# The first two column groups of a decoder's first feed-forward: weights as the resting operand, or activations

## The chip, the cores and the metric

The kernel runs on one core of a Trainium2 chip. The metric is the device time of one execution in microseconds (us), taken as the median over several executions. Beside it stands one execution that the hardware profiler recorded, with its own time and span.

## The reference

A two-layer decoder trunk on 256 tokens with a model width of 1024. Only its beginning matters here: the first half-step feed-forward of layer 0, whose inner width is 2816.

```python
def rmsnorm(x, g):
    xf = x.astype(jnp.float32)
    y = xf * lax.rsqrt(jnp.mean(xf * xf, axis=-1, keepdims=True) + EPS)
    return (y * g.astype(jnp.float32)).astype(x.dtype)

def swiglu_ffn(x, w_in, w_out):
    gate, up = jnp.split(x @ w_in, 2, axis=-1)
    return (jax.nn.silu(gate) * up) @ w_out
...
    for i in range(DEPTH):
...
        h = h + 0.5 * swiglu_ffn(rmsnorm(h, ffn1_norm[i]), ffn1_w_in[i], ffn1_w_out[i])
```

Everything else (the gated convolution, the shared keys and values, the sparse attention, the other feed-forwards) comes after it and is the same in both kernels.

## The kernel before

Every product is made in split precision: an operand is cut into a high part (rounded to the matmul type, `wh` for weights, the first 256 columns of an `xs` tile for activations) and a low part (what is left, `wl`, and the last 256 columns of `xs`). A product is high x high, low x high and high x low, added up in PSUM. ScalarE (ACT) casts the high parts, VectorE (DVE) subtracts to get the low ones. The inner dimension of 1024 is cut into eight tiles k = 0 to 7 of 128.

The instructions of each engine stand in the order in which the code is written: no scheduler moves them. So an engine that waits for one thing holds up all that stands behind it in its own queue. SP is the queue that issues nearly all DMAs, POOL adds up the squares for the norm.

Weights come as a stream `W`: `load` fetches 1 MB chunks of 2048 columns into three staging buffers `ws`; `high` and `low` cut half a chunk, a unit of 1024 columns, into `wh` and `wl`; `take`, `done` and `pump` hand units out, free them and prepare further ones, up to six ahead. For column groups a unit holds two k tiles, and a group of 256 inner features takes four units (gate and up together are 512 columns).

A feed-forward's first product is made in one of two ways.

- In `ffn_tokens` the activations rest in the array (128 tokens) and 512 weight columns move through it: per k tile two token tiles times three products, six matmuls. The result lies with tokens on partitions. `turned` applies the norm's factor per token (`rc`, from `Norm.cols`), SiLU and the gate, transposes blocks and writes them to DRAM; `placed` reads them back with features on partitions; `halved` splits them for the second product.
- For the first four tiles of 128 inner features the weights rest and the activations move: `first_tiles` makes three of them, k by k, while the input and the weights arrive in the pieces that `FIRST` and `THIRD` list; `ffn_in` makes the fourth from two units of the stream. Per tile, gate and up, and k this is one matmul of 512 columns (high weights on high and low activations) and one of 256. They need no transpose, but a factor per column (`First.rows`), sums of two halves (`total`) and an evaluation of their own (`ffn_evac`), which is woven into the groups that follow (`old`).

The column groups g = 2 to 10 then run in `ffn_tokens`, and `out_proj` follows. `NWARM` matmuls on a tile of ones run on TensorE (PE) before any input is there.

Of the kernel before, what the change touches and what calls it, by code (L numbers as in the profile page):

```python
# [9 lines left out]
F32 = mybir.dt.float32  # L10
# [6 lines left out]
P = 128  # L17
# [26 lines left out]
FROM = {"ffn1": (2, 0), "ffn2": (0, 0)}  # L44
# [25 lines left out]
def trunk(ctx, tc, A, out):  # L70
# [163 lines left out]
    w2st = mk([P, CHUNK], "ws", 3)  # L234
    came = 0
    for n, (lo, hi) in enumerate(zip(FIRST, FIRST[1:])):
        todo = [base[:, lo:hi]]
        if n in THIRD:
            todo.append(w2st[:, THIRD[n][0] * 2 * P:THIRD[n][1] * 2 * P])
        for dst in todo:  # L240
            m = P * dst.shape[1]
            (ac if came == FIRST[1] * P else sy).dma_start(dst, A["first"][came:came + m].rearrange("(p n) -> p n", p=P))
            came += m
# [4 lines left out]
    parts = {(f, g): kt8[:, g[0]:g[-1] + 1, T + f * 2 * P:T + (f + 1) * 2 * P].rearrange("p k (u m) -> p u k m", u=2)  # L248
             for f in range(2) for g in GROUPS}
    W.loaded = 3  # L250
# [122 lines left out]
    def times(r, R, n):  # L373
        ve.tensor_tensor(out=r, in0=r, in1=R[:, None, :].to_broadcast([P, n, T]), op=ALU.mult)

# [5 lines left out]

    def ffn_evac(r, R, hd):
        times(r, R, 2)
        yield
        s = t1()
        ac.activation(s, r[:, 0], AF.Silu)
        ve.tensor_tensor(out=s, in0=s, in1=r[:, 1], op=ALU.mult)
        yield
        split(s, hd)
# [12 lines left out]
    def ffn_in(xs, norm, sums):  # L402

        sums, hid, box, us, o = list(sums), [act() for _ in range(4)], [], W.take(2), bank2()
        a_pass([(o[:, x], us[x], xs, range(8)) for x in range(2)], mid=lambda: box.append(norm.rows()))
        W.done(2, False)
        sums.append(total(o, 2))
        W.pump()
        return hid, [ffn_evac(r, box[0], hd) for r, hd in zip(sums, hid)]

    def ffn_tokens(xs, norm=None, rc=None, bg=None, pre=None, n0=0, hid=(), old=()):

        hid, old, box, last = list(hid), list(old), [rc], NF // 2 - 1
# [6 lines left out]
        def turned(o):  # L420
            rc, tb = box[0], t2([P, 2, T])
            for tt in range(2):
                s = t1()
                ac.activation(s, o[:, tt, :T], AF.Silu, scale=rc[:, tt:tt + 1])  # L424
                ve.scalar_tensor_tensor(out=s, in0=o[:, tt, T:], scalar=rc[:, tt:tt + 1], in1=s, op0=ALU.mult, op1=ALU.mult)  # L425
                ve.transpose(tb[:, tt], s)  # L426
            d = mk([2, P, T], "turn", 3, pool=dr)
            sy.dma_start(d.rearrange("t p n -> p t n"), tb)
            return d

        def placed(d):
            ht = t2([P, 2, T])
            sy.dma_start(ht.rearrange("p f (c j) -> p f c j", j=32), d.rearrange("t (a i) (c f j) -> (i c) f (t a) j", i=32, f=2, j=32))
            return ht

        def halved(ht):
            for f in range(2):
                hd = act()
                split(ht[:, f], hd)
                hid.append(hd)  # L440

        ready, way = None, None
        for g in range(n0, last + 1):
            o = bank2()
            for k in range(8):
# [5 lines left out]
                for tt in range(2):  # L451
                    sh, sl = xs[k][:, tt * P:(tt + 1) * P], xs[k][:, T + tt * P:T + (tt + 1) * P]
                    pe.matmul(o[:, tt], sh, wh, start=(k == 0), stop=False)  # L453
                    pe.matmul(o[:, tt], sl, wh, start=False, stop=False)  # L454
                    pe.matmul(o[:, tt], sh, wl, start=False, stop=(k == 7))  # L455
                if k == 3 and ready is not None:
                    halved(ready)
                    ready = None
                if k == 5 and way is not None:
                    ready, way = placed(way), None  # L460
                if k == 7:
                    way = turned(o)
                    if g == last:
                        way = placed(way)
                if k % 2 == 1:
                    W.done()
                    if old and k % 4 == 1:
                        list(old.pop(0))
                    if bg is not None and k % 4 == 3:
                        bg(2 * g + k // 4)  # L470
        halved(ready)
        return hid, lambda: halved(way)

# [177 lines left out]
    sq = [t2([P, 2, T]) for _ in range(4)]  # L651

    def square(k):
        ac.activation(sq[k // 2][:, k % 2], h[k], AF.Square)

    def first_tiles():

        o = [bank2(), bank2()]
        oo, o = o, [[x[:, u] for u in range(2)] for x in o] + [[bank(), bank()]]
        w = [[mk([P, 2, 4, P], t, NBUF, F32R) for t in ("wh", "wl")] for _ in range(6)]  # L660

        def lows(f, src, g):
            wh, wl = w[2 * f + g[0] // 4]
            ks = slice(g[0] % 4, g[-1] % 4 + 1)
            ve.tensor_tensor(out=wl[:, :, ks], in0=src, in1=wh[:, :, ks].bitcast(F32), op=ALU.subtract)

        def highs(f, src, g, copy=ac.copy):
            copy(w[2 * f + g[0] // 4][0][:, :, g[0] % 4:g[-1] % 4 + 1], src)

        def product(f, k, u, x, c=slice(0, 512)):  # L670
            pe.matmul(o[f][u][:, c], w[2 * f + k // 4][x][:, u, k % 4], xs[k][:, c], start=k == x == c.start == 0, stop=(k == 7 and x == 1))

        def products(f, g):
            for x in range(2):
                for u in range(2):
                    for k in g:
                        product(f, k, u, x, slice(0, (2 - x) * T))

        def third(ks):
            g = range(*ks)  # L680
            src = w2st[:, ks[0] * 2 * P:ks[1] * 2 * P].rearrange("p (k u m) -> p u k m", u=2, m=P)
            highs(2, src, g)
            lows(2, src, g)

        def more(k):
            po.tensor_tensor(out=late if k > 1 else sq[0], in0=late if k > 2 else sq[0], in1=sq[k], op=ALU.add)

        def by_halves(k, mid):
            nm.high(k)
            highs(0, parts[0, (k,)], (k,), ve.tensor_copy)  # L690
            highs(1, parts[1, (k,)], (k,))
            nm.low(k)
            for f in range(2):
                lows(f, parts[f, (k,)], (k,))
            for c in (slice(0, T), slice(T, 512)):
                for f in range(2):
                    for u in range(2):
                        product(f, k, u, 0, c)
            mid()
            for f in range(2):  # L700
                for u in range(2):
                    product(f, k, u, 1, slice(0, T))

        by_halves(0, lambda: None)
        third(THIRD[1])
        square(0)
        products(2, (0,))
        by_halves(1, lambda: products(2, (1,)))
        square(1)
        for n, g in enumerate(GROUPS):  # L710
            if n < 2:
                continue
            for k in g:
                nm.tile(k, False)
            for f in range(2):
                highs(f, parts[f, g], g)
                lows(f, parts[f, g], g)
            for k in g:
                square(k)
            for f in range(2):  # L720
                products(f, g)
            if n == 2:
                third(THIRD[3])
            if n < 4:
                products(2, g)
            if g[-1] == 3:
                more(1)
        late = kt8[:, 6:8, 2 * T:]
        for k in (2, 3):
            more(k)  # L730
        po.tensor_tensor(out=nm.sq, in0=late[:, 0], in1=late[:, 1], op=ALU.add)
        third(THIRD[6])
        W.units += [None] * 6
        W.take(6)
        W.done(6, False)
        W.high()
        sums = [total(x, 2) for x in oo]
        products(2, GROUPS[-2] + GROUPS[-1])
        W.pump(1)
        r = t2([P, 2, T])  # L740
        for u in range(2):
            ac.copy(r[:, u], o[2][u][:, T:])
        for u in range(2):
            ve.tensor_tensor(out=r[:, u], in0=o[2][u][:, :T], in1=r[:, u], op=ALU.add)
        sums.append(r)
        W.pump(1)
        q = act()
        split(nm.sq, q)
        W.pump(2)
        return sums, q  # L750

    class First:
        def rows(self):
            pb = bank()
# [772 lines left out]
```

## Time and profile before

| what | value |
|---|---|
| median of 3 executions | 952.04 us (952.02 to 952.41) |
| the profiled execution's own time | 952.55 us |
| its span, first to last instruction | 950.8 us |
| what lies around the span | 1.75 us |
| busy share of PE, DVE, ACT, POOL | 100%, 70%, 57%, 14% |
| DMA moved over the span | 205.30 MB, mean 216 GB/s |

A busy PE is not the same as a PE at its peak: matmuls are pipelined, and a row's time for one matmul (some 390 ns) is longer than the step from one matmul to the next. Steps are read from the start times in the timeline. The profiled execution took 0.51 us more than the median of the runs.

### The profile page before, as it was taken

How to read it: one execution, taken by the hardware profiler on the slowest of the kernel's cores; microseconds unless marked ns; L12 is line 12 of the kernel's file. 1: busy time of each engine (PE TensorE's matmuls, PEld its weight loads, DVE VectorE, ACT ScalarE, POOL GpSimd, SP SyncE). 2: the span in 40 equal slices, each digit the busy share in tenths (PEclk: the TensorE clock that was granted, in tenths of full speed). 3: DMA queues.
4: the chain of work that ended last, by engine and by line, in shares of the span. 5: the costliest groups of instructions: out<-in, count | busy, mean ns of one | idle time of the engine just before them, and what ended most of it. 6: DMA issues, size and time to landing. Idle time of an engine off the chain costs nothing.

```text
span 950.8 us, 12961 instructions
## 1 busy us (share of the span) xinstructions
PE 946.1 (100%) x4712; PEld 794.8 (84%) x4712; DVE 661.1 (70%) x1066; ACT 538.5 (57%) x903; POOL 136.1 (14%) x212
## 2 busy tenths in 40 slices
PE   9999999999999999999999999999999999999998
PEld 8888888888888888888888888888877888888887
DVE  6777666778886667747757676866679787766652
ACT  7755444555565455545647774754589765445540
POOL 2000000245520100001221022200238120000000
PEclk9999999999999999999999999999999999999999
DMA  8468877645546998777646876786510248989750
GB/s 312 178 221 250 278 233 266 216 172 210 178 160 234 257 274 272 237 272 221 220 152 218 254 244 238 257 278 192 201 59 30 105 177 252 280 268 280 254 214 23
DMA packets 149467, 205.30 MB, mean 216 GB/s; under 512 B 111467, under 2 KB 126443, under 8 KB 128796
## 3 DMA queue, kind: packets, MB, share of 16 engines
q1 hardware_dynamic: 149260, 204.22, 65.7%
q8 instruction: 37, 0.61, 0.2%
q10 hardware_dynamic: 144, 0.26, 0.1%
q14 instruction: 26, 0.21, 0.1%
HBM read 189.22 MB, written 14.71 MB: 214 GB/s over the span
## 4 chain that ended last, share of the span: by engine, by line
PE 99%; ACT 0%; DVE 0%; issue 0%
PE mm L453 16%; PE mm L455 16%; PE mm L454 16%; PE a L554 7%; PE mm L355 4%; PE a L355 4%; PE a L560 4%; PE mm L516 3%; PE mm L515 3%; PE mm L514 3%; PE mm L360 2%; PE a L613 2%; PE a L612 2%; PE a L611 2%; PE a L360 2%; PE mm L1225 1%
## 5 line engine op out<-in xcount | busy, mean ns | idle before, releaser
L183 DVE TENSOR_TENSOR wl<-ws,wh 128x1024 fp32r<-128x1024 f32 x318 | 392.6, 1255 | 201.7 <-ACT wh L166 193.2
L166 ACT CAST wh<-ws 128x1024 fp32r<-128x1024 f32 x318 | 326.5, 1048 | 207.8 <-DMA ws<-in_ffn_w_in_dram 89.7
L453 PE MATMUL mm<-wh,xs 128*128 128x512 f32 x672 | 262.6, 391 | 0.0
L455 PE MATMUL mm<-wl,xs 128*128 128x512 f32 x672 | 261.7, 389 | 0.0
L454 PE MATMUL mm<-wh,xs 128*128 128x512 f32 x672 | 261.5, 389 | 0.0
L455 PEld LDWEIGHTS mm<-wl,xs 128*128 128x128 f32 x672 | 126.1, 188 | 26.8 <-DVE wl L183 0.4
L454 PEld LDWEIGHTS mm<-wh,xs 128*128 128x128 f32 x672 | 126.2, 188 | 25.8
L453 PEld LDWEIGHTS mm<-wh,xs 128*128 128x128 f32 x672 | 126.2, 188 | 25.8
L315 POOL TENSOR_TENSOR sq<-sq,t 128x256 f32<-128x256 f32 x35 | 28.5, 815 | 373.7 <-ACT t L313 373.1
L424 ACT ACTIVATE t<-mm,rc 128x256 f32<-128x256 f32 x84 | 39.7, 473 | 53.9 <-DVE t L425 46.4
L554 PE MATMUL a<-act,wh 128*128 128x512 f32 x296 | 69.5, 390 | 0.0
L554 PEld LDWEIGHTS a<-act,wh 128*128 128x128 f32 x296 | 54.9, 188 | 11.0
L514 PE MATMUL mm<-wh,act 128*128 128x512 f32 x132 | 51.3, 389 | 0.0
L515 PE MATMUL mm<-wh,act 128*128 128x512 f32 x132 | 51.3, 389 | 0.0
L516 PE MATMUL mm<-wl,act 128*128 128x512 f32 x132 | 51.3, 389 | 0.0
L425 DVE SCALAR_TENSOR_TENSOR t<-mm,rc,t 128x256 f32<-128x256 f32 x84 | 40.4, 481 | 15.4 <-ACT t L424 12.1
L363 ACT CAST act<-t 128x256 fp32r<-128x256 f32 x96 | 34.7, 404 | 27.1 <-DVE t L789 19.4
L298 ACT ACTIVATE xs<-base 128x256 fp32r<-128x256 f32 x48 | 23.8, 504 | 42.6 <-DVE base L476 29.4
L364 DVE TENSOR_TENSOR act<-t,act 128x256 fp32r<-128x256 f32 x96 | 37.1, 423 | 6.4 <-ACT act L363 6.4
L426 DVE STREAM_TRANSPOSE t<-t 128x256 f32<-128x256 f32 x84 | 37.4, 446 | 3.0
L560 PEld LDWEIGHTS a<-act,wl 128*128 128x128 f32 x296 | 37.2, 191 | 1.0
L560 PE MATMUL a<-act,wl 128*128 128x256 f32 x296 | 37.5, 283 | 0.0
(292 smaller groups left out, 1194.4 us busy)
## 6 DMA issues: line engine op xcount, KB each, us to landing
ws<-in_ffn_w_in_dram SPq DMA_DIRECT2D x85, 1024.0 KB, 5.6
ws<-in_ffn_w_out_dram SPq DMA_DIRECT2D x44, 1024.0 KB, 6.0
ws<-in_conv_w_in_dram SPq DMA_DIRECT2D x12, 1024.0 KB, 4.6
turn<-t SPq DMA_DIRECT2D x42, 256.0 KB, 2.3
t<-turn SPq DMA_DIRECT2D x42, 256.0 KB, 7.1
ws<-in_w_kv_dram SPq DMA_DIRECT2D x6, 1024.0 KB, 5.7
ws<-in_conv_w_out_dram SPq DMA_DIRECT2D x4, 1024.0 KB, 5.1
ws<-in_attn_w_q_dram SPq DMA_DIRECT2D x4, 1024.0 KB, 5.5
```

Of the source, the lines that this page charges most:

```text
L166: ac.copy(h, src)
L183: ve.tensor_tensor(out=l, in0=src, in1=h.bitcast(F32), op=ALU.subtract)
L355: pe.matmul(o, u[0][:, k * P:(k + 1) * P], xs[k], start=(k == 0), stop=False)
L425: ve.scalar_tensor_tensor(out=s, in0=o[:, tt, T:], scalar=rc[:, tt:tt + 1], in1=s, op0=ALU.mult, op1=ALU.mult)
L453: pe.matmul(o[:, tt], sh, wh, start=(k == 0), stop=False)
L454: pe.matmul(o[:, tt], sl, wh, start=False, stop=False)
L455: pe.matmul(o[:, tt], sh, wl, start=False, stop=(k == 7))
L514: pe.matmul(o[:, tt], sh, wh, start=(k == 0), stop=False)
L515: pe.matmul(o[:, tt], sl, wh, start=False, stop=False)
L516: pe.matmul(o[:, tt], sh, wl, start=False, stop=(k == NF - 1))
L554: pe.matmul(o, run[k][0], lhs[k], start=(k == 0), stop=(k == last))
L560: pe.matmul(o[:, :T], run[k][1], lhs[k][:, :T], start=False, stop=(k == last))
```

## The change

The four special tiles go. The first two column groups (the same 512 inner features) are made with the activations resting, like all others, in a function `first_groups` that works k tile by k tile on both groups at once while input and weights arrive. `PIECES` lists the loads: group 0's weights stand beside the input in `base`, group 1's lie in two of the three `ws` buffers (`second`), and two pieces, not one, are issued from ACT's queue. The sum of squares is added up by POOL tile by tile, 128x256 each (`nm.squares`), and the factor per token is made once between the two groups (`nm.cols`) instead of at the end of group 2. After k = 5, 6 and 7 one unit of the stream is prepared in between (`W.pump(1)`). The evaluations of the two groups (`turned`) come right behind each; their `placed` and `halved` are woven into groups 2 and 3.

```diff
-GROUPS = ((0,), (1,), (2,), (3,), (4, 5), (6, 7))
...
-FIRST = [0, G_N + T, G_N + KW] + [G_N + (g[-1] + 1) * KW for g in GROUPS[1:]]
-THIRD = {1: (0, 2), 3: (2, 4), 6: (4, 8)}
+PIECES = ((0, 0, G_N + T, 0), (0, G_N + T, G_N + KW, 1), (1, 0, 1, 0), (0, G_N + KW, G_N + 2 * KW, 1), (1, 1, 2, 0),
+          (0, G_N + 2 * KW, G_N + 3 * KW, 0), (0, G_N + 3 * KW, G_N + 4 * KW, 0), (1, 2, 4, 0), (0, G_N + 4 * KW, G_N + 6 * KW, 0),
+          (1, 4, 6, 0), (0, G_N + 6 * KW, G_N + 8 * KW, 0), (1, 6, 8, 0))
...
-    w2st = mk([P, CHUNK], "ws", 3)
+    second = [mk([P, CHUNK], "ws", 3) for _ in range(2)]
...
+    for which, lo, hi, queue in PIECES:
+        dst = base[:, lo:hi] if which == 0 else second[lo // 4][:, lo % 4 * 512:lo % 4 * 512 + (hi - lo) * 512]
+        m = P * dst.shape[1]
+        (sy, ac)[queue].dma_start(dst, A["first"][came:came + m].rearrange("(p n) -> p n", p=P))
+        came += m
...
-    W.loaded = 3
+    W.loaded = 4
     W.load(4)
...
-    def first_tiles():
...
+    def first_groups():
+
+        o = [[x[:, tt] for tt in range(2)] for x in (bank2(), bank2())]
+        units = {}
+        W.units += [None] * 8
+        W.at = 8
...
+        lo, hi = slice(0, T), slice(T, 512)
+        for k in range(8):
+            if k < 2:
+                nm.high(k)
+                high(0, k, ve.tensor_copy, lo)
+                high(0, k, ac.copy, hi)
+                nm.low(k)
+                high(1, k)
+                low(0, k)
+                nm.squares(k)
+                low(1, k)
+                products(0, k, 0, lo)
+                products(0, k, 0, hi)
+                for x, g in ((1, 0), (0, 1), (1, 1), (2, 0), (2, 1)):
+                    products(g, k, x)
+            else:
+                nm.tile(k)
+                for g in range(2):
+                    high(g, k)
+                    low(g, k)
+                if k < 6:
+                    for g in range(2):
+                        for x in range(3):
+                            products(g, k, x)
+            if k == 3:
+                second[0] = None
+                W.load(5)
+            if k % 2 and k < 6:
+                for g in range(2):
+                    del units[g, k // 2]
+                W.done(2, False)
+            if k > 4:
+                W.pump(1)
+        d = []
+        for g in range(2):
+            for k in (6, 7):
+                for x in range(3):
+                    products(g, k, x)
+            del units[g, 3]
+            W.done(1, False)
+            if g == 0:
+                rc = nm.cols()
+            d.append(turned(o[g], rc))
+            W.pump(2)
+        second[1] = None
+        return rc, d
...
-    sums, parts_sq = first_tiles()
-    hid, old = ffn_in(xs, First(), sums)
-    hid, rest = ffn_tokens(xs, nm, n0=2, hid=hid, old=old)
+    rc, ways = first_groups()
+    hid, came = [], []
+    old = [lambda d=d: came.append(placed(d)) for d in ways] + [lambda: halved(came.pop(0), hid) for _ in ways]
+    hid, rest = ffn_tokens(xs, rc=rc, n0=2, hid=hid, old=old)
```

`high(g, k)` casts and `low(g, k)` subtracts 512 columns; `products(g, k, x)` is two matmuls of 512 columns, x = 0 high x high, 1 low activations, 2 low weights (`wl`). The host's layout of the first weights follows. Group 2 takes two single PSUM banks, since the two double ones hold groups 0 and 1.

Where the work on the last input tiles stands in ACT's queue, before: tiles 4 and 5 are cut (`xs_119`, `xs_120`, with `wh_134` and `wh_138`), then 6 and 7, then the third tile's weights, and only then the first unit of the stream (`wh_290`, from `ws_97`).

```order
L298 ACTIVATE xs_121<-base 128x256
L298 ACTIVATE xs_122<-base 128x256
L668 CAST wh_134<-base 128x2x256
L668 CAST wh_138<-base 128x2x256
L654 ACTIVATE t_20_127<-base 128x256 x2
L668 CAST wh_142<-ws_84 128x1024
L166 CAST wh_290<-ws_97 128x1024
L369 COPY t_38_292<-mm_128 128x512
L369 COPY t_39_295<-mm_129 128x512
```

In ACT's queue after the change: tile 5 (`xs_121`), then a unit of the stream (`wh_271`, from `ws_100`, the chunk behind all first pieces), tile 6 (`xs_122`), another unit (`wh_288`), tile 7 (`xs_123`), a third unit.

```order
L644 CAST wh_234<-ws_85 128x512
L165 CAST wh_271<-ws_100 128x1024
L292 ACTIVATE xs_122<-base 128x256
L307 ACTIVATE t_39_276<-base 128x256
L644 CAST wh_280<-base 128x512
L644 CAST wh_284<-ws_85 128x512
L165 CAST wh_288<-ws_100 128x1024
L292 ACTIVATE xs_123<-base 128x256
L307 ACTIVATE t_47_295<-base 128x256
L644 CAST wh_280<-base 128x512
L644 CAST wh_284<-ws_85 128x512
L165 CAST wh_303<-ws_223 128x1024
```

What moved: the cut of input tiles 6 and 7 now stands behind casts that read `ws_100`, a chunk that SP issues behind all pieces of the input.

The same place in DVE's queue, before: the low parts of tiles 6 and 7 (`xs_121`, `xs_122`) with their weights, then the third tile's weights, two sums out of PSUM, the first unit.

```order
L302 SCALAR_TENSOR_TENSOR xs_121<-base,xs_121 128x256
L302 SCALAR_TENSOR_TENSOR xs_122<-base,xs_122 128x256
L665 TENSOR_TENSOR wl_135<-base,wh_134 128x2x256
L665 TENSOR_TENSOR wl_139<-base,wh_138 128x2x256
L665 TENSOR_TENSOR wl_143<-ws_84,wh_142 128x1024
L370 TENSOR_TENSOR t_38_292<-mm_128,t_38_292 128x512
L370 TENSOR_TENSOR t_39_295<-mm_129,t_39_295 128x512
L183 TENSOR_TENSOR wl_314<-ws_97,wh_290 128x1024
```

In DVE's queue after the change, from the first unit (`wl_273`) to the factor per token:

```order
L182 TENSOR_TENSOR wl_273<-ws_100,wh_271 128x1024
L296 SCALAR_TENSOR_TENSOR xs_122<-base,xs_122 128x256
L648 TENSOR_TENSOR wl_281<-base,wh_280 128x512
L648 TENSOR_TENSOR wl_285<-ws_85,wh_284 128x512
L182 TENSOR_TENSOR wl_292<-ws_100,wh_288 128x1024
L296 SCALAR_TENSOR_TENSOR xs_123<-base,xs_123 128x256
L648 TENSOR_TENSOR wl_281<-base,wh_280 128x512
L648 TENSOR_TENSOR wl_285<-ws_85,wh_284 128x512
L182 TENSOR_TENSOR wl_305<-ws_223,wh_303 128x1024
L340 RECIPROCAL rc_324<-sm_322 128x2
```

What moved: two subtractions of 1024 columns now stand ahead of the low weights that tile 7's last product needs.

More of the change, by code (lines that the diff above doesn't have):

```diff
@@ L380, in weave @@
             W.pump()
[L382 to L389, printed above, removed]
     def a_group(parts, xs, mid=None, late=True):
@@ L400, in a_group, with turned, placed, halved @@
         W.done(len(parts), False)
[L402 to L413, printed above, removed]
+    def turned(o, rc):
+        tb = t2([P, 2, T])
+        for tt in range(2):
+            s = t1()
+            ac.activation(s, o[tt][:, :T], AF.Silu, scale=rc[:, tt:tt + 1])
+            ve.scalar_tensor_tensor(out=s, in0=o[tt][:, T:], scalar=rc[:, tt:tt + 1], in1=s, op0=ALU.mult, op1=ALU.mult)
+            ve.transpose(tb[:, tt], s)
+        d = mk([2, P, T], "turn", 3, pool=dr)
+        sy.dma_start(d.rearrange("t p n -> p t n"), tb)
+        return d
+    def placed(d):
+        ht = t2([P, 2, T])
+        sy.dma_start(ht.rearrange("p f (c j) -> p f c j", j=32), d.rearrange("t (a i) (c f j) -> (i c) f (t a) j", i=32, f=2, j=32))
+        return ht
+    def halved(ht, hid):
+        for f in range(2):
+            hd = act()
+            split(ht[:, f], hd)
+            hid.append(hd)
+    def ffn_tokens(xs, norm=None, rc=None, bg=None, pre=None, n0=0, hid=None, old=()):
+        hid, old, box, last = [] if hid is None else hid, list(old), [rc], NF // 2 - 1
         def mid():
@@ L418, in mid @@
             box[0] = norm.cols()
[L420 to L440, printed above, removed]
         ready, way = None, None
         for g in range(n0, last + 1):
-            o = bank2()
+            if n0 and g == n0:
+                o = [bank(), bank()]
+            else:
+                o = bank2()
+                o = [o[:, tt] for tt in range(2)]
             for k in range(8):
@@ L461, in ffn_tokens @@
                 if k == 7:
-                    way = turned(o)
+                    way = turned(o, box[0])
                     if g == last:
@@ L467, in ffn_tokens @@
                     if old and k % 4 == 1:
-                        list(old.pop(0))
+                        old.pop(0)()
                     if bg is not None and k % 4 == 3:
                         bg(2 * g + k // 4)
-        halved(ready)
-        return hid, lambda: halved(way)
+        halved(ready, hid)
+        return hid, lambda: halved(way, hid)
     def out_evac(o, c, factor, norm, short=False):
@@ L649, in trunk @@
     nm = Norm([(xs, G_FFN1)])
-    sq = [t2([P, 2, T]) for _ in range(4)]
-    def square(k):
-        ac.activation(sq[k // 2][:, k % 2], h[k], AF.Square)
-    def first_tiles():
[L658 to L750, printed above, removed]
@@ L752, in trunk, with src, unit, high @@
-    class First:
-        def rows(self):
-            pb = bank()
-            for x in range(2):
-                pe.matmul(pb[:, :T], ones.bitcast(F32R), parts_sq[:, x * T:(x + 1) * T], start=(x == 0), stop=(x == 1))
-            s = t1()
-            ac.activation(s, pb[:, :T], AF.Sqrt, scale=1.0 / D, bias=epst)
-            r = mk([P, T], "R", 2)
-            ve.reciprocal(r, s)
-            return r
-    sums, parts_sq = first_tiles()
-    hid, old = ffn_in(xs, First(), sums)
-    hid, rest = ffn_tokens(xs, nm, n0=2, hid=hid, old=old)
+    def first_groups():
[3 more added lines that the diff above has]
+        W.at = 8
+        def src(g, k):
+            return second[k // 4][:, k % 4 * 512:(k % 4 + 1) * 512] if g else kt8[:, k, T:]
+        def unit(g, k):
+            if (g, k // 2) not in units:
+                units[g, k // 2] = [mk([P, 1024], t, NBUF, F32R) for t in ("wh", "wl")]
+            return [t[:, k % 2 * 512:(k % 2 + 1) * 512] for t in units[g, k // 2]]
+        def high(g, k, copy=ac.copy, q=slice(0, 512)):
+            copy(out=unit(g, k)[0][:, q], in_=src(g, k)[:, q])
+        def low(g, k):
+            wh, wl = unit(g, k)
+            ve.tensor_tensor(out=wl, in0=src(g, k), in1=wh.bitcast(F32), op=ALU.subtract)
+        def products(g, k, x, q=slice(0, 512)):
+            w = unit(g, k)[x == 2][:, q]
+            for tt in range(2):
+                c = (x == 1) * T + tt * P
+                pe.matmul(o[g][tt][:, q], xs[k][:, c:c + P], w, start=(k == x == q.start == 0), stop=(k == 7 and x == 2))
+        lo, hi = slice(0, T), slice(T, 512)
[13 more added lines that the diff above has]
+                    products(g, k, x)
+            else:
+                nm.tile(k)
[28 more added lines that the diff above has]
+        return rc, d
@@ L1487, in _layout @@
     rows = np.concatenate(cols + [rows], 1)
[L1488 to L1493 removed]
+    r["first"] = np.concatenate([(second[:, 512 * lo:512 * hi] if which else rows[:, lo:hi]).reshape(-1) for which, lo, hi, _ in PIECES])
     cols = [np.eye(128, dtype=np.float32)]
```

41 lines of the change are left out of this document (9 added, 32 removed).

## The prediction

> **What bounds the kernel now.** I read the page's head, then the waits of PE, then PE's timeline through the first 40 us.
>
> ```profile
> span 950.8 us, 12961 instructions
> PE 946.1 (100%) x4712; PEld 794.8 (84%) x4712; DVE 661.1 (70%) x1066; ACT 538.5 (57%) x903; POOL 136.1 (14%) x212
> ```
>
> ```profile
> PE a L254 <- DVE ones L229: 1.1, 1, 1.1
> PE a L1270 <- ACT xs L1280: 0.4, 1, 0.4
> ```
>
> PE is busy from its first instruction to the end, and these two are all its waits: 1.5 us in 950.8. So what the change does to the time is what it does to the moment at which PE can start group 2, plus PE work that moves across that moment. Any gap that it opens on PE is paid in full, and a faster DVE or ACT alone is worth nothing. In the timeline (start, duration, engine, line) the first stage reads:
>
> ```profile
> 4.49 2.05 PE L671 MATMUL mm<-xs,wh 128*128 128x256 f32 x8
> 6.34 0.82 PE L671 MATMUL mm<-xs,wl 128*128 128x256 f32 x4
> ...
> 7.71 1.16 PE L671 MATMUL mm<-xs,wh 128*128 128x256 f32 x8
> 8.70 0.63 PE L671 MATMUL a<-xs,wh 128*128 128x512 f32 x2
> ...
> 26.12 0.40 PE L756 MATMUL a<-act,ones 128*128 128x256 f32 x2
> 26.35 2.08 PE L360 MATMUL mm<-xs,wl 128*128 128x256 f32 x16
> 28.27 0.40 PE L453 MATMUL mm<-wh,xs 128*128 128x512 f32 x1
> ...
> 37.82 0.50 PE L342 MATMUL a<-ones,sq 128*128 128x1 f32 x4
> 38.18 0.49 PE L453 MATMUL mm<-wh,xs 128*128 128x512 f32 x1
> 38.51 0.40 PE L454 MATMUL mm<-wh,xs 128*128 128x512 f32 x1
> ```
>
> The reader is to see three things. First, the special tiles run from 4.49 to 28.27: 23.78 us. Second, eight matmuls of 256 columns step 1.85 us from 4.49, and eight of the same kind 0.99 us from 7.71: PE starts at about half its speed, which costs 0.86 here and with the next four matmuls some 1.0 us in all. Third, from 28.27 to 37.82 stand 42 matmuls of 512 columns, 9.55 / 42 = 0.2274 us each, and the factor per token costs PE 0.36 us and a late next matmul (0.33 for 0.23): 0.46 us.
>
> **PE's own sum.** The two groups are 2 x 8 x 6 = 96 matmuls of 512 columns, 21.83 us; four of them are cut in two (eight steps of 0.12 for four of 0.2274, +0.08). With the slow start as now (1.0) and the factor (0.46) PE needs 23.4 us from 4.49, and group 2 could start at 27.9, 0.4 us sooner than at 28.27. The factor then no longer stands at 37.82 (0.46 more). If PE is never kept waiting, the change gains 0.83 us. That is its ceiling: the start at 4.49 follows the warm-up matmuls, which stay.
>
> **Who feeds PE.** The steps of ACT and DVE, for two instructions in a row each:
>
> ```profile
> 11.43 0.91 ACT L298 ACTIVATE xs<-base 128x256 fp32r<-128x256 f32 x2
> 12.25 1.13 ACT L668 CAST wh<-base 128x512 fp32r<-128x512 f32 x2
> 13.28 0.72 ACT L654 ACTIVATE t<-base 128x256 f32<-128x256 f32 x2
> ...
> 24.19 2.00 ACT L166 CAST wh<-ws 128x1024 fp32r<-128x1024 f32 x2
> ```
>
> ```profile
> 13.53 1.28 DVE L665 TENSOR_TENSOR wl<-base,wh 128x512 fp32r<-128x512 f32 x2
> 14.73 0.87 DVE L302 SCALAR_TENSOR_TENSOR xs<-base,xs 128x256 fp32r<-128x256 f32 x2
> ...
> 25.50 2.35 DVE L183 TENSOR_TENSOR wl<-ws,wh 128x1024 fp32r<-128x1024 f32 x2
> 27.77 1.74 DVE L760 RECIPROCAL R<-t 128x256 f32<-128x256 f32 x1
> ```
>
> From one row's start to the next, halved: a high part of xs 0.41, a 512 cast 0.515, a square 0.31 (0.72 less its own 0.41), a 1024 cast 0.95 with 1.05 until it is done; on DVE 0.60 for 512 columns of weights, 0.40 for xs, 1.135 for 1024. One input tile with both groups' weights costs ACT 0.41 + 0.31 + 2 x 0.515 = 1.75 us and DVE 0.40 + 2 x 0.60 = 1.6 us, against PE's 12 x 0.2274 = 2.73. So up to tile 5 both run ahead of PE. Even if the second group's first weights come as late as 7.0, as a piece of 384 KB issued at 1.65 did, since they now share the way with a piece from ACT's queue, that gap at tile 0 comes before a longer one and vanishes in it.
>
> The longer one lies at the end of the stage. In ACT's queue a unit of the stream stands ahead of tile 6, and it reads chunk 4.
>
> ```profile
> 5.75 29.28 SPq L139 DMA_DIRECT2D ws<-in_ffn_w_in_dram  x7
> ws<-in_ffn_w_in_dram SPq DMA_DIRECT2D x1, 1024.0 KB, 11.2
> ...
> 7.02 12.66 SPq L139 DMA_DIRECT2D ws<-in_ffn_w_in_dram  x2
> ws<-in_ffn_w_in_dram SPq DMA_DIRECT2D x1, 1024.0 KB, 12.4
> ```
>
> Each timeline row is an issue, the row beneath it its size and time to landing: chunk 3 lands at 16.95, chunk 4 at 19.4, 2.45 us per MB. Before, 4144 KB of first pieces and chunk 3 went ahead of chunk 4; now 5168 KB of first pieces do. That is the same sum, so I take 19.4 again. ACT has done tile 5 by about 17 and then stands.
>
> DVE's work also meets POOL, which now adds 128x256 squares for every tile while DVE reads two tiles from SBUF. The rows that show such a meeting:
>
> ```profile
> L302 DVE SCALAR_TENSOR_TENSOR xs<-base,xs x8: 471/477/1233, 4.2 to 15.1; 128x256 fp32r<-128x256 f32 x8
> ```
>
> ```profile
> 11.40 1.53 POOL L686 TENSOR_TENSOR t<-t,t 128x512 f32<-128x512 f32 x1 [7.43 <-ACT t L654]
> ...
> 20.55 0.74 POOL L731 TENSOR_TENSOR sq<-base 128x256 f32<-128x256 f32 x1
> ```
>
> ```profile
> 11.97 1.63 DVE L302 SCALAR_TENSOR_TENSOR xs<-base,xs 128x256 fp32r<-128x256 f32 x2 [0.20 <-ACT xs L298]
> ```
>
> ```profile
> 175.72 1.00 POOL L315 TENSOR_TENSOR sq<-sq,t 128x256 f32<-128x256 f32 x1 [5.13 <-ACT t L313]
> ```
>
> ```profile
> 175.70 1.30 DVE L535 SCALAR_TENSOR_TENSOR base<-t,base 128x256 f32<-128x256 f32 x2
> ```
>
> Seven of eight xs subtractions take about 0.48 us; the one that starts at 11.97, inside POOL's add, takes 1.23: 0.76 more. At 175.7 an add of just the kind that is coming takes 1.00 in place of 0.74, and two subtractions 1.30, where two steps of 0.40 would end after some 0.75: 0.55 more. The change has one such add beside tile 6 and one beside tile 7 on the path. Each costs DVE between 0 and 0.76; I take 0.55, the row of the same kind and size. The Trainium skill's "SBUF — State Buffer" has a rule for this, in its part on the shared port pair: VectorE with two SBUF inputs and GpSimd exclude each other for a whole instruction. The trace agrees in kind (1.23 for 0.48); held for the whole 0.74 us add twice, the forecast below would be 0.4 us later.
>
> **The chain that sets group 2's start.** Chunk 4 lands at 19.40; ACT's cast is done at 20.48; DVE takes its low part, free at 21.64. Tile 6: xs 0.40 + 0.55, weights 2 x 0.60, free at 23.79. The second unit 1.135: 24.93. Tile 7: xs 0.40 + 0.55, first weights 0.68 to their end: 26.56. ACT stays ahead: 19.43 + 0.95 + 1.75 + 0.95 + 0.41 + 0.31 + 0.62 puts tile 7's first cast at 24.4. PE, which could have reached this product at about 24.5, has the two last matmuls of group 0 left: 27.0. Then the factor, 0.46, and twelve matmuls of group 1, 2.73: group 2 starts at 30.2. Against 28.27 that is 1.92 later; less the 0.46 that no longer stands at 37.82, **+1.46 us**.
>
> **The other parts, costed at nothing.** `ffn_evac`, `total` and two loads of ACT's table leave ACT and DVE; PE waited for none of them. The evaluations of groups 0 and 1 stand behind unit 10 in ACT's and DVE's queues and run from about 28 to 35; they hold PSUM that PE wants back at group 3, near 41. Units 11 to 13 stand behind them, and PE wants unit 11 at 30.2 + 3 x 2.73 = 38.4. If that cover went, PE would wait for a unit's cast, 1 us. SP issues four more DMAs, two writes and two reads of the turned tiles, between the chunks:
>
> ```profile
> turn<-t SPq DMA_DIRECT2D x42, 256.0 KB, 2.3
> t<-turn SPq DMA_DIRECT2D x42, 256.0 KB, 7.1
> 40.00:50.00 10.00, 10.00 (x46) 8.27 (x45) 5.88 (x11) 6.49 (x9) 0.00 (x0) 1.00 0.04 13
> ```
>
> At most 2 x (2.3 + 7.1) = 19 us of transfer time on a path that in this stretch is 4% busy, with units prepared six ahead (16 us of PE). Chunk 6 waits on SP for the last reader of `second[1]`, at about 27, lands some 5 us later and is wanted at 41. The writes stand ahead of chunk 7 and 8 on SP and hold them until the evaluations are done; PE wants chunk 7 at 46.6.
>
> **Measure.** The sum is made in the profiled execution: a span of 950.8 + 1.46 = 952.2, its own time 952.55 + 1.46 = 954.0. That execution stood 0.51 above the median, so against 952.04 I predict 953.5. A measurement of this kernel tells about 0.2%, 1.9 us, from no change: 950.1 to 953.9 is the same.
>
> **Rivals.**
>
> 1. *POOL and DVE miss each other.* If each add falls into a gap or takes DVE's turn at the price of zero, tile 7's weights are ready 1.1 sooner: +0.36, 952.4. For it: at 20.55 POOL's add took its plain 0.74. Against it: DVE stands nowhere between 20.5 and 28 in the chain, so an add has no gap to fall into.
> 2. *Slower: chunk 4 comes later.* The chain hangs on one landing, and its price is one to one. From a landing at 19.85 on (0.45 later) the change is slower by over 0.2%; at 20.4 it is 954.5. For it: one MB more comes as small first pieces, and the piece of 384 KB above needed until 7.0, so the way in is not always full. Against it: as many bytes as before, issued early enough to queue without a break.
> 3. *PE is never kept waiting.* Then 951.2, still the same by the bound. For it: tile by tile ACT and DVE need 1.75 and 1.6 us against 2.73. Against it: chunk 4's place ahead of tile 6 in ACT's queue. Only if the slow start went as well (1.0) would it come near a gain of 0.2%. This is also how it ends if the change does nothing but trade one order of operands for another.
>
> **How the numbers follow.** The chain as summed 0.52 (953.0 to 953.9, with POOL's price between 0.3 and 0.76), rival 1 0.20, rival 2 0.22, rival 3 0.06. Rival 2 and a sliver of the chain's upper end are slower: 0.24; rival 3 gives 0.03 to faster; the rest, 0.73, is the same. The range reaches half a microsecond under rival 1, for a chunk 4 that lands that much earlier, and over rival 2's 954.5 a little: 951.9 to 954.7; it leaves out rival 3 and a landing after 20.6.
>
> **What would show it.** In the profile after: PE's waits list some 2 us in the first 30, on DVE's `wl` and `xs` of tile 7 and on ACT's `wh`; ACT stands for DMA `ws` from about 17 to 19.4 before the first unit; xs subtractions of tiles 6 and 7 take about 1 us; group 2's first matmul starts near 30.2; no PE wait later. Wrong if PE has no wait, if the waits lie at tiles 0 or 1, or if group 2 starts before 28.5 or after 31.

## The result, and the profile after

| | before | after |
|---|---|---|
| median of 6 executions each | 952.17 us (951.81 to 952.59) | 957.62 us (957.25 to 958.11) |
| ratio, 95% interval | | 1.0056 [1.0045, 1.0066] |
| the profiled execution, its span | 952.55, 950.8 us | 957.79, 956.0 us |

The change makes the kernel slower by 5.45 us (0.56%). The prediction was 953.5 within 951.9 to 954.7, with 0.73 on no change: the size is wrong, and so is the likeliest sign. One execution among the experiments (of e2_before_64) took 1352.24 us at a granted clock of 0.655 and is left out of that run's ratio.

The head of the page after, and PE's waits, which were nearly nothing before:

```profile
span 956.0 us, 12889 instructions
PE 949.5 (99%) x4674; PEld 790.7 (83%) x4674; DVE 657.8 (69%) x1058; ACT 532.8 (56%) x895; POOL 138.2 (14%) x215
```

```profile
PE a L248 <- DVE ones L228: 1.1, 1, 1.1
PE mm L654 <- ACT wh L644: 0.8, 2, 0.5
PE mm L654 <- DVE xs L296: 0.7, 1, 0.7
PE a L1211 <- ACT xs L1221: 0.4, 1, 0.4
PE mm L654 <- ACT xs L292: 0.4, 1, 0.4
```

Two things do not fit each other. The new waits are 0.8 + 0.7 + 0.4 = 1.9 us, all in the first stage. But PE is also *busy* for 3.4 us longer (949.5 for 946.1) with 38 matmuls fewer. So most of the loss is no wait at all.

The first stage, PE's timeline after (start, duration, engine, line; the bracket is the idle time ahead of it and what ended it):

```profile
4.89 1.22 PE L654 MATMUL mm<-wh,xs 128*128 128x256 f32 x6 [0.35 <-ACT xs L292]
6.64 1.21 PE L654 MATMUL mm<-wh,xs 128*128 128x512 f32 x4 [0.53 <-ACT wh L644]
...
23.99 0.73 PE L654 MATMUL mm<-wh,xs 128*128 128x512 f32 x2 [0.24 <-ACT wh L644]
25.43 0.73 PE L654 MATMUL mm<-wh,xs 128*128 128x512 f32 x2 [0.70 <-DVE xs L296]
26.03 0.73 PE L654 MATMUL mm<-wl,xs 128*128 128x512 f32 x2
26.59 0.50 PE L336 MATMUL a<-ones,sq 128*128 128x1 f32 x4
...
29.77 0.39 PE L430 MATMUL a<-wh,xs 128*128 128x512 f32 x1
```

Group 2 starts at 29.77 (forecast 30.2, before 28.27). From there on the same matmuls can be laid side by side in the two traces. At 39 us, with the factor per token gone from group 2, after is 0.98 us behind. The distance then grows, and only in some stretches: to 2.69 at 427 us, 3.54 at 648, 5.25 at 945. These stretches are the second products of the feed-forwards, where an `act` tile rests in the array: `out_proj` with rest (L514 to L516 before, L491 to L493 after) and `out_last` (L611 to L613, now L588 to L590). The first and the last row of one run of 73 matmuls there, before:

```profile
410.29 0.39 PE L515 MATMUL mm<-wh,act 128*128 128x512 f32 x1
...
426.61 0.39 PE L515 MATMUL mm<-wh,act 128*128 128x512 f32 x1
```

and the same 73 after:

```profile
412.50 0.40 PE L492 MATMUL mm<-wh,act 128*128 128x512 f32 x1
...
429.30 0.40 PE L492 MATMUL mm<-wh,act 128*128 128x512 f32 x1
```

72 steps took 16.32 us before, 226.7 ns each, and take 16.80 now, 233.3 ns. In the groups by line (x count | busy us, mean ns of one | idle us before) the same shows as a longer matmul, with no idle time in front of it. Before:

```profile
L453 PE MATMUL mm<-wh,xs 128*128 128x512 f32 x672 | 262.6, 391 | 0.0
L554 PE MATMUL a<-act,wh 128*128 128x512 f32 x296 | 69.5, 390 | 0.0
L514 PE MATMUL mm<-wh,act 128*128 128x512 f32 x132 | 51.3, 389 | 0.0
L611 PE MATMUL a<-wh,act 128*128 128x512 f32 x86 | 33.5, 389 | 0.0
L861 PE MATMUL a<-wh,kt 128*128 128x512 f32 x16 | 6.3, 395 | 0.0
L861 PE MATMUL a<-wh,t 128*128 128x512 f32 x16 | 6.2, 391 | 0.0
```

After:

```profile
L430 PE MATMUL mm<-wh,xs 128*128 128x512 f32 x656 | 256.2, 391 | 0.0
L531 PE MATMUL a<-act,wh 128*128 128x512 f32 x296 | 70.0, 392 | 0.0
L491 PE MATMUL mm<-wh,act 128*128 128x512 f32 x132 | 52.2, 396 | 0.0
L588 PE MATMUL a<-wh,act 128*128 128x512 f32 x86 | 34.0, 396 | 0.0
L802 PE MATMUL a<-wh,kt 128*128 128x512 f32 x16 | 6.3, 395 | 0.0
L802 PE MATMUL a<-wh,t 128*128 128x512 f32 x16 | 6.3, 395 | 0.0
```

The reader is to see which lines moved. In these names the moving tile stands first and the resting one second. Where `xs` rests, 391 stays 391. Where `act` rests, 389 becomes 396, though neither the code, the shapes nor the order of these lines changed. And the profile before already held the same pair in one line: at L861 one and the same matmul takes 395 ns with `kt` resting and 391 with `t` (a `t2` tile), which after takes 395 as well.

What did change is where `act` lies. The tiles of one pool are laid out in SBUF in the order of their first use. Before, the norm's small tiles `sm` and `rc` (24 x 96 + 2 x 32 = 2368 bytes of a partition) are first used behind `act`; the change uses them in `first_groups`, ahead of `t2` and `act`; the six `t1` tiles, 6144 bytes, come ahead of `act` too, but move it by a multiple of 1024. From the programs as built: `act` begins at byte 145408 before, a multiple of 1024, and at 153920 after, 64 bytes past a multiple of 256; `t2` ahead of it and `pr` and `R` behind it are 64 off as well. `xs`, `wh` and `wl` stay on multiples of 1024. `kt`, the slow one at L861, lies 64 bytes off before too.

### The profile page after: what moved, and what is told of

It reads as the page before. It is cut to its first block, busy times and chain, and to the rows that moved or that the text cites. A ratio compares the mean times of both kernels' runs of the same rounds, so it can differ in the third digit from the quotient of the medians.

```text
span 956.0 us, 12889 instructions
## 1 busy us (share of the span) xinstructions
PE 949.5 (99%) x4674; PEld 790.7 (83%) x4674; DVE 657.8 (69%) x1058; ACT 532.8 (56%) x895; POOL 138.2 (14%) x215
## 4 chain that ended last, share of the span: by engine, by line
PE 95%; DVE 2%; DMA 2%; issue 0%; ACT 0%; SPq 0%; DVEq 0%; ACTq 0%
PE mm L430 16%; PE mm L432 16%; PE mm L431 15%; PE a L531 7%; PE mm L349 4%; PE a L537 4%; PE mm L491 3%; PE mm L492 3%; PE mm L493 3%; PE a L349 3%; PE a L588 2%; PE a L589 2%; PE a L590 2%; PE mm L354 2%; PE a L354 2%; PE mm L1166 1%
## 5 line engine op out<-in xcount | busy, mean ns | idle before, releaser
L430 PE MATMUL mm<-wh,xs 128*128 128x512 f32 x656 | 256.2, 391 | 0.0
L432 PE MATMUL mm<-wl,xs 128*128 128x512 f32 x656 | 255.4, 389 | 0.1
L431 PE MATMUL mm<-wh,xs 128*128 128x512 f32 x656 | 255.2, 389 | 0.0
L432 PEld LDWEIGHTS mm<-wl,xs 128*128 128x128 f32 x656 | 123.2, 188 | 26.3 <-DVE wl L182 0.5
L431 PEld LDWEIGHTS mm<-wh,xs 128*128 128x128 f32 x656 | 123.2, 188 | 25.3
L430 PEld LDWEIGHTS mm<-wh,xs 128*128 128x128 f32 x656 | 123.2, 188 | 24.9
L309 POOL TENSOR_TENSOR sq<-sq,t 128x256 f32<-128x256 f32 x42 | 35.8, 853 | 386.8 <-ACT t L307 386.1
L491 PE MATMUL mm<-wh,act 128*128 128x512 f32 x132 | 52.2, 396 | 0.0
L493 PE MATMUL mm<-wl,act 128*128 128x512 f32 x132 | 52.2, 395 | 0.0
```

The source lines that it names most:

```text
L430: pe.matmul(o[tt], sh, wh, start=(k == 0), stop=False)
L431: pe.matmul(o[tt], sl, wh, start=False, stop=False)
L432: pe.matmul(o[tt], sh, wl, start=False, stop=(k == 7))
L493: pe.matmul(o[:, tt], sh, wl, start=False, stop=(k == NF - 1))
```

## The experiments

Every comparison below is with the kernel before on the same chip. "Step" is the mean distance from one matmul's start to the next one's, over all matmuls of a line, without gaps over 300 ns.

**1. The change with its old places (e1_align).** `rc` is given rows of 384 bytes, so that all behind it lies on multiples of 1024. Nothing else differs.

```diff
-            r = mk([P, 2], "rc", 2)
+            r = mk([P, 96], "rc", 2)[:, :2]
```

> The changed kernel, with the two rc tiles made 384 bytes long each, so that t2 and act, which lie behind sm and rc in SBUF, start at a multiple of 1024 bytes again, as act did before the change. Nothing else differs. Theory P (place in SBUF): the 6.5 ns that every matmul with a resting act tile lost (233.3 for 226.8) come back; some 660 such matmuls, so 957.6 - 4.2 = 953.4, and the step in the second product is 226.8 again. Rival S (the extra comes along with the new order: two more turned groups, other buffers for the hidden tiles, more DMAs): nothing changes, 957.6 and a step of 233.3.

Measured 952.86 us against 952.63, ratio 1.0005 [0.9997, 1.0014]. 5.2 us of the change's 5.45 are gone with this one edit. (In the two profiles 4.9 us are, and 0.3 of these lie in the first stage, where group 2 starts at 29.46 and not 29.77 because chunk 4 came that much sooner in this execution: ACT casts it from 18.64 on, from 18.97 in after.)

```profile
L491 PE MATMUL mm<-wh,act 128*128 128x512 f32 x132 | 51.3, 389 | 0.0
L588 PE MATMUL a<-wh,act 128*128 128x512 f32 x86 | 33.5, 389 | 0.0
L802 PE MATMUL a<-wh,kt 128*128 128x512 f32 x16 | 6.2, 390 | 0.0
```

`kt` has come to a multiple of 1024 here, and its matmul went from 395 to 390. That repairs a place that was off in the kernel before as well: PE's distance to before falls from 0.68 us at 40 to 0.31 at 485, behind the lines with `kt`.

**2. The kernel before with `act` 64 bytes off (e2_before_64).** The other way round: a tile of 64 bytes goes ahead of `act`.

```diff
     def first_tiles():
...
+        po.memset(mk([P, 16], "gap", 1), 0.0)
+
         def lows(f, src, g):
```

> The kernel before, with one unused tile of 64 bytes ahead of act, so that act lies 64 bytes off a multiple of 1024, and the order of work as before. P: the step with a resting act tile goes from 226.8 to about 233 and the time to 952.2 + 4.3 = 956.5. S: 952.2, step 226.8. If only the full distance of the changed kernel (320 bytes) does harm, also 952.2.

Measured 956.91 us, ratio 1.0046 [1.0033, 1.0059]. So 64 bytes, with no change to the work, make the old kernel 4.3 us slower:

```profile
L514 PE MATMUL mm<-wh,act 128*128 128x512 f32 x132 | 52.2, 396 | 0.0
L611 PE MATMUL a<-wh,act 128*128 128x512 f32 x86 | 34.0, 396 | 0.0
```

The sum agrees: 396 matmuls at L514 to L516 and 258 at L611 to L613, by 6.6 ns each, are 4.3 us; where `act` moves instead, 296 steps of 512 columns grow by 1.6 ns and 296 of 256 columns shrink by 2.0, which cancels.

**3. What holds up the first stage (e3_late_units, e4_no_adds).** Both stand on e1_align. The first prepares the three stream units behind the loop over k instead of inside it, so that tiles 6 and 7 no longer stand behind casts that read chunk 4:

```diff
-            if k > 4:
-                W.pump(1)
+        W.pump(3)
```

> As e1_align, but the three units of the stream are prepared after input tile 7 and not after tiles 5, 6 and 7. Chain theory (ACT and DVE come to tiles 6 and 7 only after chunk 4 has landed): PE's waits at tiles 6 and 7 go, group 2 starts near 28.2 and not at 29.8, and the time is 1.6 below e1_align, 951.8 if P holds. Rival D (the input's own last pieces or DVE's work on tiles 0 to 5 hold PE up): group 2 stays near 29.8, no difference to e1_align.

Measured 951.14 us, ratio 0.9985 [0.9977, 0.9994]: 1.72 us off e1_align. PE's waits, and in its timeline the start of group 2:

```profile
PE a L248 <- DVE ones L228: 1.0, 1, 1.0
PE a L1210 <- ACT xs L1220: 0.4, 1, 0.4
```

```profile
27.73 0.39 PE L430 MATMUL a<-wh,xs 128*128 128x512 f32 x1
```

Every wait of the first stage but the warm-up's is gone, the one at tile 0 too, and group 2 starts at 27.73, where e1_align has 29.46. The wait at tile 0 was not what the edit touched; it came and went between executions (0.5 in after, 0.6 in e1_align, 1.1 in e4_no_adds, none here). In the three that have it PE was at full speed by 4.9 us and came to the second group's first product before its weights were cast; here PE reached full speed only at about 6.2.

The second leaves the units where they were and drops POOL's additions for tiles 6 and 7:

```diff
-                nm.tile(k)
+                nm.tile(k, k < 6)
+                if k > 5:
+                    ac.activation(t1(), h[k], AF.Square)
```

> As e1_align, but the squares of input tiles 6 and 7 are computed and not added to the sum (this leaves a quarter of the sum of squares out of the first norm). Theory L (POOL's add and DVE's subtraction of two SBUF tiles exclude each other): xs of tiles 6 and 7 takes 0.48 on DVE and not 0.96, PE gets tile 7's operands 1.0 us sooner, and the time is 0.9 to 1.0 below e1_align: 952.4 if P holds. Rival: the xs subtractions still take 0.96, no difference to e1_align.

Measured 951.97 us, ratio 0.9994 [0.9986, 1.0003]: 0.89 us off e1_align for two additions. DVE's timeline after, at tiles 6 and 7:

```profile
21.19 0.97 DVE L296 SCALAR_TENSOR_TENSOR xs<-base,xs 128x256 fp32r<-128x256 f32 x1
...
24.42 0.95 DVE L296 SCALAR_TENSOR_TENSOR xs<-base,xs 128x256 fp32r<-128x256 f32 x1
```

POOL's in after at that place:

```profile
20.88 1.00 POOL L309 TENSOR_TENSOR sq<-sq,t 128x256 f32<-128x256 f32 x1 [4.90 <-ACT t L307]
23.57 1.51 POOL L309 TENSOR_TENSOR sq<-sq,t 128x256 f32<-128x256 f32 x1 [1.70 <-ACT t L307]
```

and DVE's with the additions gone:

```profile
20.96 0.48 DVE L296 SCALAR_TENSOR_TENSOR xs<-base,xs 128x256 fp32r<-128x256 f32 x1
...
23.70 0.48 DVE L296 SCALAR_TENSOR_TENSOR xs<-base,xs 128x256 fp32r<-128x256 f32 x1
```

0.97 and 0.95 become 0.48: 0.48 us for each addition, and both sides pay, since POOL's own took 1.00 and 1.51. This is the exclusion that the Trainium skill's "SBUF — State Buffer" tells of in its part on the shared port pair; the runs put its price for this pair of instructions at 0.45 to 0.49 us on the path, less than a whole addition of 0.74.

**4. Which address counts (f1, f2, f3, f5, f6).** All are the kernel before with gaps of other sizes or at other places; one execution each, the profiled one. The kernel before itself lay between 951.72 and 953.24 us in 29 executions, so a single time says little, and the steps carry the argument. For an offset of `act` and of what lies behind it (`kt` among it, but neither `xs` nor the weights) the edit of e2_before_64 with 8, 32, 64 or 112 floats in place of 16:

> The kernel before with 32 bytes ahead of act. A resting block is 128 columns of 4 bytes, 512 bytes of a partition; with act on a multiple of 1024 each block begins on a multiple of 512. Theory B (the cost is there whenever a resting block crosses a boundary of 512 bytes, however little of it): 231 to 235 ns, about 956.7, as with 64 and 128 bytes. Theory S (the cost grows with what is cut off the end): half of that of 64 bytes, about 230 ns and 954.7.

> The kernel before with 128 bytes in place of 64 set ahead of act. Theory L (what costs is that the resting tile starts inside a 128-byte stretch of a partition): act lies on such a boundary again, the steps in out_proj with rest and in out_last are 226.7 ns, the time that of before, about 952.6. Theory K (the boundary is longer, 256, 512 or 1024 bytes, since act lay on a multiple of 1024 before): the steps are 233.3 ns as with 64 bytes, the time about 956.9.

> The kernel before with 256 bytes ahead of act, so that each resting block begins in the middle between two multiples of 512. Theory B (boundary of 512 bytes): 231 to 235 ns, about 956.9. Theory Q (boundary of 256 bytes; 128 bytes did cost): the steps are 226.7 and the time 952.6 again. Theory S (cost by the part cut off): more than with 128 bytes, over 235 ns, above 958.

> The kernel before with 448 bytes ahead of act, 64 bytes short of the next multiple of 512. Theory B and theory Q: 231 to 235 ns, about 956.9, as with 64 bytes, since a block crosses a boundary. Theory S, if only the part behind the boundary counts: far above 235 ns; if the smaller part counts: as with 64 bytes.

Measured, with the kernel before at 952.63 beside 64, at 952.52 beside 128 and at 952.88 beside the other three:

| `act` past a multiple of 1024 by | step L514–516 | step L554, `act` moves, 512 | step L560, `act` moves, 256 | time |
|---|---|---|---|---|
| 0 (before) | 226.7 ns | 227.6 | 119.7 | |
| 32 bytes | 233.3 | 233.3 | 117.2 | 957.37 us |
| 64 (e2) | 233.3 | 229.2 | 117.7 | 956.91 |
| 128 | 232.4 | 232.8 | 119.2 | 957.06 |
| 256 | 226.7 | 227.6 | 119.7 | 952.33 |
| 448 | 228.9 | 233.2 | 115.6 | 953.05 |

The group rows, in this order: 128 bytes,

```profile
L514 PE MATMUL mm<-wh,act 128*128 128x512 f32 x132 | 52.1, 395 | 0.0
```

256 bytes,

```profile
L514 PE MATMUL mm<-wh,act 128*128 128x512 f32 x132 | 51.3, 389 | 0.0
```

and 448 bytes:

```profile
L515 PE MATMUL mm<-wh,act 128*128 128x512 f32 x132 | 52.0, 394 | 0.0
L514 PE MATMUL mm<-wh,act 128*128 128x512 f32 x132 | 51.7, 392 | 0.0
L516 PE MATMUL mm<-wl,act 128*128 128x512 f32 x132 | 51.2, 388 | 0.0
```

At 256 bytes each line's mean is back at what it was with `act` on 1024, so it is multiples of 256 bytes that are free; the boundaries of theories L (128) and B (512) fall, K holds in its smallest size alone, and Q's 256 stands. A flat price for whatever lies off does not: 448 bytes, 192 past a multiple of 256, cost only 2.2 ns in the mean, and unevenly by line. Theory S of these four texts, a price that grows with what is cut off, falls too: 32 bytes cost as much as 64, and 128 no more. Where `act` moves (L554) the prices are as high as where it rests, but at other offsets: 64 bytes cost little there, and 448 the full price.

Then `xs` alone (`gap` ahead of it, 960 bytes behind, so that all else keeps its place):

```diff
     w2st = mk([P, CHUNK], "ws", 3)
+    po.memset(mk([P, 16], "gap", 1), 0.0)
...
     xs = new_xs()
+    po.memset(mk([P, 240], "gap2", 1), 0.0)
```

> The kernel before with 64 bytes ahead of xs and 960 behind it, so that xs alone (and gap) lies 64 bytes off and every tile behind it keeps its place on a multiple of 1024. Theory L (any resting tile that starts 64 bytes off): the 2016 matmuls of 512 columns in which xs rests in the feed-forwards' first products step 233.3 ns in place of 226.7, 13.3 us more in all, about 966 us with the few other places where xs rests; out_proj with rest, where act rests, stays at 226.7. Theory A (it is something about act, such as what DVE and ACT write beside it, and not the start address of what rests): 226.7 in both places, about 952.6.

Measured 965.37 us against 952.52, 12.85 more. The first products, not the second, are slow now (the code stands one line lower):

```profile
L454 PE MATMUL mm<-wh,xs 128*128 128x512 f32 x672 | 266.3, 396 | 0.0
...
L515 PE MATMUL mm<-wh,act 128*128 128x512 f32 x132 | 51.4, 389 | 0.0
```

The steps of the three lines with resting `xs` are 233.3 ns for 226.9 before: 2016 x 6.4 = 12.9 us, the whole difference. So theory A, that it is something about `act`, falls: a resting `xs` pays the same.

Last the weights alone, 64 bytes off, with the two gaps around `wh` and `wl`:

```diff
+        po.memset(mk([P, 16], "gap", 1), 0.0)
         w = [[mk([P, 2, 4, P], t, NBUF, F32R) for t in ("wh", "wl")] for _ in range(6)]
+        po.memset(mk([P, 240], "gap2", 1), 0.0)
```

> The kernel before with 64 bytes ahead of wh and wl and 960 behind them, so that the weights alone lie 64 bytes off. They move where xs and act rest, and rest where act or xs moves. Theory L (the resting tile's own address): steps with resting xs and act stay near 226.7 to 227 (a moving tile 64 bytes off was seen to cost about 1.6 ns at 512 columns where act moved and to save 2 at 256); where 512 columns of act move over resting wh, 227.6 becomes about 233. In all 3 to 9 us more, most of it where the weights rest. Theory D (what counts is that the resting and the moving tile lie differently against the boundary): the steps of 2016 matmuls with resting xs and 650 with resting act go to 233.3, 17 us more, about 970.

Measured 959.10 us, 6.6 more, within theory L's 3 to 9 and far from theory D's 17. But the steps are not those of theory L:

```profile
L453 PE MATMUL mm<-wh,xs 128*128 128x512 f32 x672 | 264.9, 394 | 0.0
L454 PE MATMUL mm<-wh,xs 128*128 128x512 f32 x672 | 261.5, 389 | 0.0
L554 PE MATMUL a<-act,wh 128*128 128x512 f32 x296 | 71.1, 394 | 0.0
...
L514 PE MATMUL mm<-wh,act 128*128 128x512 f32 x132 | 51.7, 392 | 0.0
...
L863 PE MATMUL a<-wh,kt 128*128 128x512 f32 x16 | 6.2, 390 | 0.0
```

Where the weights rest (L554), 227.6 becomes 233.1 ns, as theory L has it, and the 256 columns of L560 go from 119.7 to 115.6. Where they move over an aligned `xs`, the three lines' steps are 230.6, 226.8 and 229.7, 2.1 ns more in the mean; by 2016 that is 4.2 us, where theory L had next to nothing. Where they move over an aligned `act` (L514 to L516) the mean is 228.9. And `kt`, which rests 64 bytes off here just as in the kernel before (the two gaps add up to 1024), is no longer slow: its three lines fall from 233.4 to 228.1 (L861 before, L863 here, 395 to 390), about the 228.3 that it has in e1_align, where it is aligned. What changed for it is that the weights that move over it are 64 bytes off as well.

So the resting tile's address alone, theory L, does not explain the steps. What theory D had in mind does: how the resting and the moving tile lie to each other. Its price was wrong, since it took 233.3 for every difference. Sorted by resting start less moving start, modulo 256 bytes, the steps of 512 columns at L514 to L516, at L554 and of the lines in which `xs` or `kt` rests are these:

| difference | step | where |
|---|---|---|
| 0 | 226.7 ns | `act` rests, 0 or 256 bytes off |
| 0 | 228.0, 228.1 | `kt` rests, in f6_before_448 and in f5_weights_64 |
| 32 | 233.3 | `act` rests, 32 off |
| 64 | 233.3, 233.3, 233.4 | `act` (e2), `xs` (f3) or `kt` (before) rests, 64 off |
| 64 | 233.1, 233.2 | weights rest 64 off; `act` moves 448 off |
| 96 | 233.7 | `kt` rests in f2_before_32 |
| 128 | 232.4, 233.1, 232.8 | `act` rests 128 off; `kt` rests in e2; `act` moves 128 off |
| 192 | 228.9, 229.2 | `act` rests 448 off; `kt` rests in f1_before_128 |
| 192 | 229.2, 229.0, 228.9 | `act` moves 64 off; weights move 64 off over `xs`, over `act` |
| 224 | 233.3 | `act` moves, 32 off |

By these rows it does not matter which of the two tiles is off. This reading came after the runs, and none was made to test it; `kt` in f5_weights_64 is the row that theory L cannot have. A short stretch does not fit: at L355, 16 matmuls that move an aligned `t` over aligned weights step 232.9 ns in the kernel before. Why a difference of 192 costs less than one of 224 or 128 stays open.

**5. The better version (f4_one_piece).** e3_late_units with the input's tile 1 issued by SP again:

```diff
-... (0, G_N + KW, G_N + 2 * KW, 1), ...
+... (0, G_N + KW, G_N + 2 * KW, 0), ...
```

> The aligned change with the three stream units prepared after the last tile (951.14 before), and the input's tile 1 issued from SP again, so that a single piece goes by ACT's queue. If the two pieces on ACT's queue share the way with the second group's first weights and make them late (waits of 0.6 to 1.1 us at tile 0 in three of the runs, none in the run with late units), the second group's first product no longer waits: up to 0.6 us off in such executions, about 950.8 in the median. If ACT's queue only moved the input's tile 1 ahead and SP is then a piece (0.6 us of issue) later for all pieces behind, tile 1 is late instead: the same 951.1, or up to 0.6 more.

Measured 951.00 us against 952.52, ratio 0.9984 [0.9975, 0.9993]. That is e3_late_units' ratio of 0.9985 again, so the piece's queue is worth nothing that shows. In its profile ACT casts the second group's first weights from 4.65 on, in e3_late_units from 5.38, but it then stands 0.74 us for tile 1; PE, at half speed until 7.2, waited for neither. Both versions beat both kernels, by 0.15% over the one before; by the PE starts of e3_late_units, 1.05 of its 1.5 us come from the first stage and 0.37 from the lines with `kt`.

## Why the prediction was wrong, point by point

**What bounds the kernel: half right.** PE is the bound. But "what the change does to the time is what it does to the moment at which PE can start group 2, plus PE work that moves across that moment" is the step that failed. It took PE's work behind that moment as fixed because its instructions are the same. The third way to lose time is that the same instructions each take longer, and nothing in the sum had a term for that. **"The other parts, costed at nothing"** listed DVE's, ACT's and SP's work, and left out that the new place of `nm.cols` also moves the first use of `sm` and `rc`, and with it the place of every tile first used after them. That term is 654 matmuls x 6.6 ns = 4.3 us; the change's whole price is 5.45, and the chain's 1.0 below is most of the rest.

**The chain that sets group 2's start: right, one term off.** ACT stood for chunk 4, DVE's low parts came in the forecast order, and tile 7's `xs` was the last wait:

```profile
18.97 1.05 ACT L165 CAST wh<-ws 128x1024 fp32r<-128x1024 f32 x1 [2.85 <-DMA ws<-in_ffn_w_in_dram]
```

The cast starts at 18.97, not 19.40; group 2 at 29.77, not 30.2. Both are 0.43 early, so the steps between, worked out from rows of before, hold: each is within 0.2 us, and their misses cancel. The landing was mis-sized. The term came to +1.0 for a forecast of +1.46. That it hung on this chain is shown by e3_late_units, which takes it away.

**POOL against DVE: right in kind, a little high.** 0.55 was taken for each addition; the subtractions grew by 0.48 and the run without the additions gained 0.45 each.

**"That gap at tile 0 comes before a longer one and vanishes in it": right.** PE lost 0.35 and 0.53 there, and the chain on chunk 4 still set the end.

**The slow start: a constant that was none.** The sum took the 1.0 us of PE's slow start in before as given. By the steps in the traces full speed came at 6.7 us in before, but at 4.0 in after, still within the warm-up matmuls, and at 4.8 in e1_align. It did not move the end of after's first stage, since the chain waited anyway. Without that wait it shows: e3_late_units, at full speed from about 6.2, starts group 2 at 27.73, 0.87 us later than 4.49 plus the 22.37 that the matmuls need by the prediction's sum without its slow start, and f4_one_piece, at full speed from 7.2, at 28.23. Not all of the 0.87 could be won, by an estimate from these rows: a PE at full speed would have come to the second group's first product at about 5.4, and ACT's cast for it ended at 6.0.

**Rivals.** Rival 3, never kept waiting, gave 951.2; e3_late_units, which is that case with the tiles in place, measured 951.14. That the two nearly agree is luck: the gain was forecast as 0.83 and is 1.49 against its own kernel before, 0.37 of it from the lines with `kt`. Rivals 1 and 2 did not occur: the additions did meet DVE, and chunk 4 was early.

**What would show it.** The waits on tile 7's `xs` and ACT's `wh`, ACT's stand and the two long subtractions all appeared, and no wait came later. "No PE wait later" was true and said nothing, since the loss behind 30 us is not a wait.

## What to carry to other kernels

When a change adds a small tile, or uses one earlier, look at where the big tiles behind it end up in SBUF, and whether those that rest in the array and those that move over them still lie a multiple of 256 bytes apart: here 64 bytes cost more than all the work that was moved. Compare the mean time and the start-to-start step of matmuls that the change did *not* touch; a busy total that grows with fewer instructions, and no wait, points there. An instruction row that takes 395 ns beside an identical one of 391 is a finding in the profile before, not noise.

## What the runs showed of the hardware that was not expected

A matmul of 512 fp32 columns stepped 226.7 ns when its resting 128x128 block and its moving tile began a multiple of 256 bytes of the partition apart, and 232.4 to 233.3 when the resting one began 32, 64, 128 or 224 bytes past that; 192 past cost about 2.2 ns. The weight load's own rows do not show it, before and after alike 188 ns. Before:

```profile
L514 PEld LDWEIGHTS mm<-wh,act 128*128 128x128 f32 x132 | 24.8, 188 | 5.1
```

and after:

```profile
L491 PEld LDWEIGHTS mm<-wh,act 128*128 128x128 f32 x132 | 24.8, 188 | 5.9
```

The Trainium skill's "SBUF — State Buffer" speaks, under "Specifications (TRN2)", of cachelines of 16 bytes, with a penalty for each crossing to a new one; an offset of 32 bytes crosses no more of those, and yet it cost 6.6 ns, so the runs show something that this line size doesn't tell. Its section "Operand start alignment" says of its own measurements that they are about legality and timed nothing, so the price here stands beside it, not against it.

At 256 columns (L560) the same offsets of the moving `act` saved 0.5 to 4.1 ns. No run explains the saving.

The moment at which PE reaches full speed at the start varied between 4.0 us (after) and 7.2 (f4_one_piece) with the same warm-up matmuls. The Trainium skill's "TensorE: Matmul & The Clock Gate" says in its Part 1 that this moment is run-variable; these traces agree.
